# Block products of the second projections with the contraction pairs outside and the result's quarters inside, in chunks of up to seven pairs, and an entry that makes all blocks of u before their differences

## The chip, the cores and the metric

The kernel runs on one core of a Trainium2 chip. The metric is the device time of one execution in microseconds. A NeuronCore has TensorE (PE in the profile, with its weight loads as PEld), VectorE (DVE), ScalarE (ACT), GpSimd (POOL) and SyncE (SP), which here issues most transfers. Each engine works through its own list of instructions in order and waits where an instruction's inputs, or the buffer that it writes, are not ready.

## What is computed

A network of two blocks on x of 1024 rows (tokens) by 1024 columns, all in float32. The first block has two layers, each a mixer and an MLP; the second has a mixer and a gated feed-forward part. The change touches the two MLPs and the feed-forward part:

```python
# layer = 0, 1
u = x * (1.0 + scale) + shift
y = jnp.square(jax.nn.relu(u @ mlp_w1[layer] + mlp_b1[layer])) @ mlp_w2[layer] + mlp_b2[layer]
x = layer_norm(ALPHA * x + gate * y, ln_g[layer, 1], ln_b[layer, 1])
# second block
h = _causal_depthwise_conv(x @ w_up, conv_f_w, conv_f_b)
g, val = h[..., :2816], h[..., 2816:]
x = _layernorm(ALPHA2 * x + (jax.nn.silu(g) * val) @ w_down, ln2_g, ln2_b)
```

`mlp_w1` is 1024 by 4096, `w_up` 1024 by 5632; `mlp_w2` is 4096 by 1024 and `w_down` 2816 by 1024. In the text "first products" are those with `mlp_w1` and `w_up`, "second products" those with `mlp_w2` and `w_down`.

## The kernel before

Every float32 operand of a product is split into a high part (rounded, made by an ACT copy) and a low part (the rest, made by a DVE subtraction), and a product is three matmuls: high by high, high by low, low by high. One instruction list per engine is written out by hand in program order; what is issued earlier on an engine is done earlier on it.

**The entry** (`boundary`, L580) leads into each first product. It finishes the previous product with `last_sums`, normalises the rows, and then makes the transposed operand u, by halves h (512 tokens) and blocks kt (128 columns): `u_tile` (L570) is four transposes on PE into a `pb` bank, an affine ACT pass into `ur`, an ACT copy for the high part and a DVE subtraction for the low part. There are two `pb` buffers. The blocks of h = 1 are made while PE computes the h = 0 halves of the second and third of three weight tiles (`pss[1]`, `pss[2]`), at set places between the matmuls. After that come the h = 1 halves of all three, which need the blocks of h = 1, then a fourth weight tile (`fm_unit`), then the first block products (`FmProducts`). Those need, beside u itself, differences of the blocks of u: `diffs` (L1261) makes eight DVE operations and four ACT copies for one j of 0 to 3, out of the blocks j and j + 4 of both halves, into two tiles `t`. In the kernel before, `diffs` is issued right after the later of the two blocks, between the `u_tile` calls. Three entries have differences: those of the two MLPs and of the feed-forward part. In the last, the evacuations `evacs` hold a convolution, two DVE operations on 1024 columns each, and a product.

**The second products** (`TmProducts`, L1375) take the 2 by 2 block scheme with seven products instead of eight. Contraction blocks of 128 rows are taken in pairs. A chunk is a group of pairs over which a product is summed in PSUM before it is added to the result in SBUF (`acc`). There are 4, 3, 3 and 4 pairs in an MLP's chunks and 3, 3 and 3 in the feed-forward part's. For each chunk and each of the seven products j, `run` (L1466) goes over the four quarters t of the result (128 rows by 512 columns), and inside a quarter over the m pairs of the chunk, three matmuls each: 12 m matmuls for a product. `split` (L1433) makes the operands `he` of the next product beside this one (an ACT copy and a DVE subtraction for every two pairs, once for the weights `rw` and once for the hidden blocks `rh`), `sums` (L1417) the differences of weight blocks on DVE, four per chunk, and `add` (L1494) adds the finished halves of a product to `acc` on DVE: eleven additions of 1024 columns and six of 512 for a chunk. In the first chunk the first write of each quadrant of `acc` is an ACT copy instead, seven of 1024 and two of 512.

Beside the products run a side job, `residual_job` (L1504: load a row tile `zt`, two DVE operations, store, eight times), in the MLPs also `gated` (four weight tiles times the gate), and in the last chunk `ws.split` of the eight tiles for the entry after, and `add_residual` (L1519), which for each quadrant twice loads `zi`, in the MLPs multiplies `acc` by the gate on POOL, and adds `zi` on DVE. `step` (L1692) sets when. `begin` (L1648) makes the first loads and splits during the last pair of the first products.

SBUF tiles come from two pools: 21 buffers `W8` of 8 KB per partition (u, t, `he`, `rw`, `acc`, weight tiles) and 7 buffers `T4` of 4 KB (`rh`, `zt`, `zi`, `st`). PSUM has three buffers `ps` of two banks and two `pb` of one. A tile waits until a buffer is free.

Of the kernel before, what the change touches and what calls it, by code (L numbers as in the profile page):

```python
# [9 lines left out]
F32 = mybir.dt.float32  # L10
# [244 lines left out]
def tile_net(ctx: ExitStack, tc: tile.TileContext, x, wts, ada, adag, cols, rows, sfm, rgw, wup, wsp, out):  # L255
# [324 lines left out]
    def boundary(hs, wsx, xres, G, B, keys, evacs, spill=None, ops=None):  # L580
# [794 lines left out]
    class TmProducts:  # L1375
# [4 lines left out]

        def __init__(self, name, chunks, fresh):
            self.name, self.chunks, self.fresh = name, chunks, fresh
            self.n = 7 * len(chunks)
            self.w, self.h, self.ent = {}, {}, {}
            self.loaded, self.did = set(), set()
            self.nx = 0
# [4 lines left out]
        def weights(self, c, i, f):  # L1391

            if c >= len(self.chunks) or (c, i, f) in self.w:
                return
            ps = self.chunks[c]
            t = self.w[c, i, f] = W8("rw", (128, 4, 512), F32)
            u = _UNITS[self.name, 2 * ps[0]]
            src = wts[u:u + 2 * len(ps)].rearrange("(q two) p n -> two p q n", two=2)[i]
            nc.sync.dma_start(out=t[:, 0:len(ps), :], in_=src[:, :, f * 512:(f + 1) * 512])

        def load(self, g, k_):

            if g >= self.n or 2 * k_ >= self.m(g) or (g, k_) in self.loaded:
                return
            self.loaded.add((g, k_))
            c, j = divmod(g, 7)
            n = min(2, self.m(g) - 2 * k_)
            p = self.chunks[c][2 * k_]
            t = self.h[g, k_] = T4("rh").rearrange("p (q n) -> p q n", q=2)
            nc.sync.dma_start(out=t[:, 0:n, :], in_=d_h[p:p + n, (0, 6, 1, 2, 3, 4, 5)[j]].rearrange("q p n -> p q n"))  # L1410

        def w_of(self, g):

            c, j = divmod(g, 7)
            return self.w[(c,) + ((0, 0), (1, 0), (0, 0), (0, 0), (1, 1), (0, 1), (0, 0))[j]]

        def sums(self, g):  # L1417
            while self.nx <= min(g, self.n - 1):
                c, j = divmod(self.nx, 7)
                m = len(self.chunks[c])  # L1420
                x, b12, b22, b21 = [self.w[(c,) + k_][:, 0:m, :] if (c,) + k_ in self.w else None
                                    for k_ in ((0, 0), (0, 1), (1, 1), (1, 0))]
                if j == 2:
                    tt(x, b12, x, SUB)
                elif j == 3:
                    tt(x, b22, x, SUB)
                elif j == 4:
                    tt(b12, b22, b12, SUB)
                elif j == 6:
                    tt(x, b21, x, SUB)  # L1430
                self.nx += 1

        def split(self, g, k_):  # L1433

            if g >= self.n or 2 * (k_ % 2) >= self.m(g) or (g, k_) in self.did:
                return
            self.did.add((g, k_))
            q, n = 2 * (k_ % 2), min(2, self.m(g) - 2 * (k_ % 2))
            if k_ >= 2:
                self.sums(g)  # L1440
# [1020 lines left out]
```

## Time and profile before

| what | value |
|---|---|
| runs | 3709.20, 3709.82, 3719.66 us (median 3709.82) |
| profiled execution | 3706.28 us, its span 3704.4 us |
| PE busy | 3515.9 us, 95% of the span |
| DVE busy | 2663.2 us, 72% |
| ACT, POOL busy | 1469.9 us, 568.2 us |

The profile is one execution, seen by engine. A PE timeline merges matmuls that follow each other without a pause; the number in brackets is the idle time ahead of a row and what released it. A busy PE may still be slow, when its clock was granted at less than full speed. Averages over the span hide that the stages differ; so windows of a stage are read beside the timeline.

### The profile page before, as it was taken

To read this page: it belongs to the slowest core of one execution; us is meant where nothing else is said; L and a number is where in the kernel's file an instruction comes from. 1 tells how busy PE (TensorE), PEld (TensorE's weight loads), DVE (VectorE), ACT (ScalarE), POOL (GpSimd) and SP (SyncE) were. 2 spreads that over 40 slices of the span, in tenths; PEclk is the share of its full clock that TensorE was granted. 3 is DMA by queue.
4 is the path that set the end of the run, shared out by engine and by line. 5 is a ranking of instruction groups with operands and counts; after the bars stand their busy time and mean duration, and the time that the engine had idled before them with its cause. 6 is when DMAs were issued, how large, how long until landed. Compare 5 with 4: busy or idle time off the path is not lost. (4 is left out here: it accounts for less than half of the span.)

```text
span 3704.4 us, 43629 instructions
## 1 busy us (share of the span) xinstructions
PE 3515.9 (95%) x17098; PEld 2864.4 (77%) x17098; DVE 2663.2 (72%) x3640; ACT 1469.9 (40%) x1957; POOL 568.2 (15%) x415
## 2 busy tenths in 40 slices
PE   7999899999999999999899999999989999999997
PEld 5877778887877778888787888877768677777765
DVE  5574767868997764454647666798889677877897
ACT  4254353343335442443425334432413354444431
POOL 2002113300022000000202331002200013322002
PEclk9999999999999999999999999999989999999998
DMA  6343235465642222100122445574210323222662
GB/s 228 109 135 122 80 129 190 174 229 199 238 132 93 71 81 81 46 30 30 67 93 104 149 148 213 190 264 137 100 54 29 125 76 110 88 87 104 222 218 91
DMA packets 184160, 469.16 MB, mean 127 GB/s; under 512 B 15601, under 2 KB 20353, under 8 KB 183954
## 3 DMA queue, kind: packets, MB, share of 16 engines
q1 hardware_dynamic: 177378, 446.35, 34.1%
q0 software_dynamic: 6576, 20.03, 1.6%
q8 instruction: 134, 2.20, 0.2%
q14 instruction: 72, 0.59, 0.0%
HBM read 340.99 MB, written 125.32 MB: 126 GB/s over the span
## 5 line engine op out<-in xcount | busy, mean ns | idle before, releaser
L247 PE MATMUL ps<-u,wu 128*128 128x512 f32 x2880 | 755.6, 408 | 13.9 <-ACT u L577 5.3
L247 PEld LDWEIGHTS ps<-u,wu 128*128 128x128 f32 x2880 | 533.0, 192 | 140.1 <-issue 14.0
L247 PE MATMUL ps<-he 128*128 128x512 f32 x2442 | 582.9, 397 | 28.0 <-DVE he L305 21.7
L247 PEld LDWEIGHTS ps<-he 128*128 128x128 f32 x2442 | 460.6, 190 | 144.6 <-DVE he L305 33.0
L247 PE MATMUL ps<-t,we 128*128 128x512 f32 x1728 | 423.5, 393 | 5.4 <-DVE cc L305 5.3
L247 PEld LDWEIGHTS ps<-t,we 128*128 128x128 f32 x1728 | 323.4, 188 | 83.3 <-DVE cc L305 8.8
L247 PE MATMUL pb<-u,we 128*128 128x512 f32 x1152 | 281.9, 393 | 0.0
L247 PE MATMUL ps<-wu,u 128*128 128x256 f32 x1920 | 262.5, 291 | 16.4 <-DVE wu L218 14.3
L247 PEld LDWEIGHTS ps<-wu,u 128*128 128x128 f32 x1920 | 243.0, 193 | 27.4 <-DVE wu L218 15.1
L247 PEld LDWEIGHTS pb<-u,we 128*128 128x128 f32 x1152 | 216.2, 188 | 49.5 <-DVE we L305 0.2
L1446 ACT CAST he<-rw 128x1024 fp32r<-128x1024 f32 (+1 forms) x154 | 132.7, 911 | 240.4 <-DVE rw L305 227.0
L247 PE MATMUL ps<-pw,wu 128*128 128x512 f32 x816 | 211.3, 407 | 14.5 <-DVE xres L308 8.8
L1925 DVE TENSOR_REDUCE mx<-ps 128x1 f32<-128x128 f32 (+7 forms) x128 | 95.6, 755 | 173.5 <-PE ps L247 173.1
L305 DVE TENSOR_TENSOR we<-sf,we 128x512 fp32r<-128x512 f32 x192 | 153.9, 814 | 85.7 <-ACT we L1339 84.7
L305 DVE TENSOR_TENSOR he<-rw,he 128x1024 fp32r<-128x1024 f32 (+1 forms) x154 | 162.6, 1098 | 61.4 <-ACT he L1446 61.2
L1965 ACT ACTIVATE p<-ps 128x1024 f32<-128x1024 f32 (+7 forms) x128 | 82.9, 649 | 304.2 <-PE ps L247 288.4
L247 PEld LDWEIGHTS ps<-pw,wu 128*128 128x128 f32 x816 | 155.0, 194 | 51.5 <-DVE xres L308 9.2
L305 DVE TENSOR_TENSOR he<-rh,he 128x1024 fp32r<-128x1024 f32 (+1 forms) x154 | 165.9, 1079 | 18.6 <-ACT he L1446 18.4
L1446 ACT CAST he<-rh 128x1024 fp32r<-128x1024 f32 (+1 forms) x154 | 136.5, 911 | 88.5 <-DMA rh<-d_h 81.7
L305 DVE TENSOR_TENSOR acc<-acc,ps 128x1024 f32<-128x1024 f32 (+1 forms) x148 | 154.1, 1042 | 17.0 <-PE ps L247 16.6
L305 DVE TENSOR_TENSOR we<-wx,we 128x512 fp32r<-128x512 f32 x144 | 134.3, 934 | 44.5 <-ACT we L1339 44.5
L247 PE MATMUL pb<-he 128*128 128x512 f32 x666 | 158.5, 392 | 0.0
(395 smaller groups left out, 5847.7 us busy)
## 6 DMA issues: line engine op xcount, KB each, us to landing
st<-in_wts_dram SPq DMA_DIRECT2D x108, 512.0 KB, 3.4
rh<-d_h SPq DMA_DIRECT2D x105, 512.0 KB, 5.4
sf<-in_wts_dram SPq DMA_DIRECT2D x96, 512.0 KB, 6.6
d_h<-hx SPq DMA_DIRECT2D x37, 1024.0 KB, 5.1
d_h<-rr SPq DMA_DIRECT2D x111, 256.0 KB, 2.3
sta<-in_ada_dram SPq DMA_DIRECT2D x48, 512.0 KB, 3.6
rw<-in_wts_dram SPq DMA_DIRECT2D x28, 768.0 KB, 6.1
sta<-in_adag_dram SPq DMA_DIRECT2D x32, 512.0 KB, 3.9
```

Of the source, the lines that this page charges most:

```text
L247: return self.eng.matmul(out=out, lhsT=lhsT, rhs=rhs, **kw)
L305: (eng or dve).tensor_tensor(out=o, in0=a, in1=b, op=op)
L1446: act.copy(d[:, 0, 0:n, :], src)
L1925: dve.tensor_reduce(out=mx[:, t:t + 1], in_=ps[:, 0:n], axis=AX.X, op=ALU.max)
L1965: act.activation(out=p[:, 128 * i:1024], in_=ps[:, 128 * i:1024], func=AF.Exp)
```

## The change

At the three entries with differences the calls of `diffs` leave the place between the blocks of h = 1. The first is issued within the h = 1 half of the first weight tile, the second after it, the third after the second tile and its predecessor's evacuation, the fourth after the third tile.

In the second products the chunks become 7 and 7 pairs (MLPs) and 5 and 4 (feed-forward part). Inside a product the loop over the pairs is outside, two at a time (a unit), and the four quarters inside, so that a quarter gets 6 matmuls at a time, 3 in a unit of one pair, and all four quarters of a product end in its last unit. The additions to `acc` follow there, all at once. The order of the seven products changes so that those that accumulate in the two `aa` buffers (j = 0, 2, 4, 6) alternate with those in `cc` and the `pb` banks. Operands are split two units ahead and loaded four units ahead. The weights of a chunk come in two tiles per block, of up to four pairs. `begin` and `step` are spread anew over the units.

```diff
-                    if kt > 3 and ops is not None:
-                        diffs([[raws[h, kt - 4 + 4 * a] for a in range(2)] for h in range(2)], ops)
+        def diff(j):
+            if ops is not None:
+                diffs([[raws[h, j + 4 * a] for a in range(2)] for h in range(2)], ops)
+
         for c, _ in enumerate(fm_mms(pss[0], w[0], uT, 1)):
             if c % 2:
                 residual(4 + c // 2)
+            if c == 3:
+                diff(0)
+        diff(1)
         ws.split(ws.ng + 1, True, lo=pool)
         run(fm_mms(pss[1], w[1], uT, 1))
         evacs[0](pss[0])
+        diff(2)
         run(fm_mms(pss[2], w[2], uT, 1))
+        diff(3)
         evacs[1](pss[1])
...
+        def split(self, upto):
+            while self.ns < min(upto + 1, len(self.units)):
+                u = self.ns
+                (g, q), n = self.units[u], len(self.pairs(u))
+                c, j = divmod(g, 7)
+                if q % 2 == 0:
+                    self.sums(c, j, q // 2)
+                self.load(u)
...
+                for src in (self.w[(c,) + at + (q // 2,)][:, o:o + n, :], self.h.pop(u)[:, 0:n, :]):
+                    d = W8("he", (128, 2, 2, 512))
+                    act.copy(d[:, 0, 0:n, :], src)
+                    tt(d[:, 1, 0:n, :], src, d[:, 0, 0:n, :].bitcast(F32), SUB)
...
         def run(self, xres, step):
...
+                for q in range(0, m, 2):
+                    self.split(u + 2)
+                    self.load(u + 4)
+                    dw, dh = self.ent.pop(u)
+                    n = min(2, m - q)
+                    for t in range(4):
+                        s_ = slice(t * 128, (t + 1) * 128)
+                        for i in range(n):
...
+                    step(g, q // 2)
+                    u += 1
+                if on_a:
+                    for h in range(2):
+                        self.add(xres, c, j, 2 * h, 2, aa[h])
+                else:
+                    self.add(xres, c, j, 0, 2, cc[0])
+                    for t in (2, 3):
+                        self.add(xres, c, j, t, 1, cc[t - 1])
...
-            tp = TmProducts(f"w2_{l}", [[0, 1, 2, 3], [4, 5, 6], [7, 8, 9], [10, 11, 12, 13]], True)
+            tp = TmProducts(f"w2_{l}", [[0, 1, 2, 3, 4, 5, 6], [7, 8, 9, 10, 11, 12, 13]], True)
...
+        def step(g, q):
             c, j = divmod(g, 7)
+            last = g >= tp.n - 7
+            if g > 1 and not (last and j > 2):
+                for _ in range(2 if last or gate is None else 1):
+                    next(side_work, None)
+            if last:
+                if (j, q) == (3, 0):
+                    run(side_work)
+                if q == 1 and j > 3:
+                    add_residual(xres, gate, *((0, 1), (1, 1), (0, 0))[j - 4])
+                ws.split(min(ws.ng + 8, max(ws.ns, ws.ng + (0, 1, 2, 3, 3 + q, 7, 8)[j])))
...
-        tp = TmProducts("dn", [[0, 1, 2], [3, 4, 5], [6, 7, 8]], True)
+        tp = TmProducts("dn", [[0, 1, 2, 3, 4], [5, 6, 7, 8]], True)
```

## Rows read from the trace of the kernel before

**Rows 1.** The page, busy time: engine, us, share of the span, instructions.
```profile
PE 3515.9 (95%) x17098; PEld 2864.4 (77%) x17098; DVE 2663.2 (72%) x3640; ACT 1469.9 (40%) x1957; POOL 568.2 (15%) x415
```

**Rows 2.** Windows, one of 20 us in a three-pair chunk: busy time, clock, DMA.
```profile
900.00:920.00 20.00, 18.94 (x81) 14.55 (x80) 19.93 (x21) 3.95 (x6) 0.00 (x0) 1.00 0.64 233
```

**Rows 3.** Timeline of PE, first entry: start, length, matmuls, [idle before, releaser].
```profile
462.42 8.56 PE L247 MATMUL ps<-u,wu 128*128 128x512 f32 x36
470.81 0.60 PE L251 MATMUL pb<-ident,xres 128*128 128x128 f32 x4
...
480.00 0.66 PE L251 MATMUL pb<-ident,xres 128*128 128x128 f32 x4 [2.38 <-ACT ur L576]
...
495.79 25.57 PE L247 MATMUL ps<-u,wu 128*128 128x512 f32 x110 [0.23 <-DVE u L305]
521.21 2.96 PE L247 MATMUL ps<-u,we 128*128 128x512 f32 x12
```

**Rows 4.** Timeline of all engines at the first wait of that entry.
```profile
475.36 0.69 DVE L305 TENSOR_TENSOR tx<-ur 128x512 f32<-128x512 f32 x1
...
476.08 1.35 ACT L1274 CAST t<-tx 128x512 fp32r<-128x512 f32 x2 [1.36 <-DVE tx L305]
...
479.18 0.77 ACT L576 ACTIVATE ur<-pb,gb 128x512 f32<-128x512 f32 x1
479.22 1.29 DVE L305 TENSOR_TENSOR t<-ur,t 128x512 fp32r<-128x512 f32 x2
...
480.50 0.77 ACT L576 ACTIVATE ur<-pb,gb 128x512 f32<-128x512 f32 x1
```

**Rows 5.** Windows, 8 us around that wait (columns as in rows 2).
```profile
478.00:486.00 8.00, 4.77 (x17) 3.56 (x17) 7.17 (x13) 5.63 (x10) 0.00 (x0) 0.79 0.00 0
```

**Rows 6.** Timeline of PE, third entry: the same two places.
```profile
2985.84 8.33 PE L247 MATMUL ps<-u,wu 128*128 128x512 f32 x36
...
3044.45 2.92 PE L247 MATMUL ps<-u,we 128*128 128x512 f32 x12
```

**Rows 7.** Timeline of PE, start and end of the three stages of second products.
```profile
795.98 4.35 PE L247 MATMUL ps<-he 128*128 128x512 f32 x18
...
1075.42 8.48 PE L247 MATMUL ps<-wl,wu 128*128 128x512 f32 x36
...
2301.33 8.94 PE L247 MATMUL ps<-he 128*128 128x512 f32 x38
...
2587.56 8.53 PE L247 MATMUL ps<-wl,wu 128*128 128x512 f32 x36
...
3439.83 8.75 PE L247 MATMUL ps<-he 128*128 128x512 f32 x37
...
3632.49 12.69 PE L247 MATMUL ps<-wl,wu 128*128 128x512 f32 x54
```

**Rows 8.** Groups by shape, DVE, first stage of second products: busy us, mean ns.
```profile
L305 DVE TENSOR_TENSOR he<-rh,he 128x1024 fp32r<-128x1024 f32 x40 | 51.0, 1274 | 4.6 <-ACT he L1446 4.5
L305 DVE TENSOR_TENSOR acc<-acc,ps 128x1024 f32<-128x1024 f32 x36 | 43.8, 1217 | 3.5 <-PE ps L247 3.4
L305 DVE TENSOR_TENSOR rw<-rw 128x2048 f32<-128x2048 f32 x7 | 16.0, 2284 | 0.0
L305 DVE TENSOR_TENSOR acc<-acc,pb 128x512 f32<-128x512 f32 x22 | 15.0, 683 | 0.7 <-PE pb L247 0.7
```

**Rows 9.** Timeline of all engines, last chunk of the second stage.
```profile
2546.72 0.80 PE L247 MATMUL ps<-he 128*128 128x512 f32 x1 [3.54 <-DVE he L305]
...
2573.77 3.30 POOL L305 TENSOR_TENSOR acc<-acc,gate 128x1024 f32<-128x1024 f32 x1 [4.56 <-DVE acc L305]
2574.74 3.40 DVE L305 TENSOR_TENSOR he<-rh,he 128x1024 fp32r<-128x1024 f32 x1
```

**Rows 10.** Groups of the whole span, a convolution step of the feed-forward part.
```profile
L308 DVE SCALAR_TENSOR_TENSOR rr<-cc,col,rr 128x1023 f32<-128x1023 f32 x20 | 26.3, 1314 | 26.3 <-ACT rr L2304 26.3
```

More of the change, by code (lines that the diff above doesn't have):

```diff
@@ L1383, in __init__ @@
             self.n = 7 * len(chunks)
+            self.units = [(g, q) for g in range(self.n) for q in range((self.m(g) + 1) // 2)]
             self.w, self.h, self.ent = {}, {}, {}
-            self.loaded, self.did = set(), set()
-            self.nx = 0
+            self.nl = self.ns = 0
         def m(self, g):
@@ L1391, in weights @@
         def weights(self, c, i, f):
-            if c >= len(self.chunks) or (c, i, f) in self.w:
+            if c >= len(self.chunks) or (c, i, f, 0) in self.w:
                 return
[L1395 to L1431, printed above, removed]
@@ L1449, in beside @@
-        def beside(self, g, t):
-            if t == 0:
-                self.split(g + 1, 2)
-                self.split(g + 1, 3)
-            elif t < 3:
-                self.split(g + 1, t - 1)
-            else:
-                self.sums(g + 2)
-        def fetch(self, g, t):
-            c, j = divmod(g, 7)
-            if t > 1:
-                self.load(g + 2, t - 2)
-            elif t == 0 and 1 < j < 6:
-                self.weights(c + 1, *((0, 0), (1, 0), (0, 1), (1, 1))[j - 2])
+            for x in range(0, len(self.chunks[c]), 4):
+                ps = self.chunks[c][x:x + 4]
+                t = self.w[c, i, f, x // 4] = W8("rw", (128, 4, 512), F32)
+                u = _UNITS[self.name, 2 * ps[0]]
+                src = wts[u:u + 2 * len(ps)].rearrange("(q two) p n -> two p q n", two=2)[i]
+                nc.sync.dma_start(out=t[:, 0:len(ps), :], in_=src[:, :, f * 512:(f + 1) * 512])
@@ new lines, in pairs, with load @@
+        def pairs(self, u):
+            g, q = self.units[u]
+            return self.chunks[g // 7][2 * q:2 * q + 2]
+        def load(self, upto):
+            while self.nl < min(upto + 1, len(self.units)):
+                ps = self.pairs(self.nl)
+                j = (0, 1, 2, 3, 4, 6, 5)[self.units[self.nl][0] % 7]
+                t = self.h[self.nl] = T4("rh").rearrange("p (q n) -> p q n", q=2)
+                nc.sync.dma_start(out=t[:, 0:len(ps), :], in_=d_h[ps[0]:ps[0] + len(ps), j].rearrange("q p n -> p q n"))
+                self.nl += 1
@@ L1472, in run @@
                     aa = [PSUM(), PSUM()]
[L1473 removed]
+                if j in (1, 5):
                     cc = [PSUM(), PB(), PB()]
[L1475 to L1492 removed]
@@ new lines, in run @@
+                on_a, start = j % 2 == 0, j in (0, 1, 5)
+                os_ = [aa[t // 2][:, t % 2 * 512:t % 2 * 512 + 512] if on_a else
+                       cc[0][:, t * 512:(t + 1) * 512] if t < 2 else cc[t - 1] for t in range(4)]
+                for q in range(0, m, 2):
[6 more added lines that the diff above has]
+                        for i in range(n):
+                            first, last = start and q + i == 0, q + i == m - 1
+                            hh, hl, wh, wl = dh[:, 0, i, s_], dh[:, 1, i, s_], dw[:, 0, i, :], dw[:, 1, i, :]
+                            pe.matmul(out=os_[t], lhsT=hh, rhs=wh, start=first, stop=False, skip_group_check=not start)
+                            pe.matmul(out=os_[t], lhsT=hh, rhs=wl, start=False, stop=False, skip_group_check=not start)
+                            pe.matmul(out=os_[t], lhsT=hl, rhs=wh, start=False, stop=last, skip_group_check=not start)
+                    if q == 0:
+                        if j in (0, 1):
+                            self.weights(c, 1, 1 - j)
+                        elif j in (5, 6):
+                            self.weights(c + 1, 0, j - 5)
+                    step(g, q // 2)
+                    u += 1
```

81 lines of the change are left out of this document (25 added, 56 removed).

## The prediction

> **What bounds the kernel.** I read the page's busy times first: PE is busy 95% of the span [rows 1], so a gain can only come from places where PE stands still or runs at its lower clock. The PE timeline of the stages that the change touches comes next. A matmul of 512 columns takes 0.231 us from start to start: 110 of them fill 495.79 to 521.21 [rows 3].
>
> At the first entry PE goes from 462.42 to 521.21, 58.8 us [rows 3]. The work in it is 192 matmuls (four weight tiles of 48), 44.4 us, and eight groups of four transposes. A group moves what follows by about 0.35 us: the matmuls ahead of it end by their pitch at 462.42 + 36 x 0.231 = 470.74, and of its 0.60 us [rows 3] a good part overlaps. That makes 2.8 us, and 58.8 - 47.2 = 11.6 us are lost. The timeline says how: PE waits 2.4 us for an ACT pass `ur` [rows 3], twice, and 1.7 us a third time, and after a wait the granted clock averages 0.79 [rows 5], part of the time at 1.2 instead of 2.4 GHz. ACT is late because `diffs` stands in its list between two blocks of u: its copy waits 1.36 us for DVE's `tx`, and the next block's `ur` starts only at 479.18 [rows 4], while PE has run out of `pb` buffers. The pattern repeats at the other two entries; the third takes 2985.84 to 3044.45, 58.6 us, so 11.4 lost [rows 6], and the second lies between them.
>
> The three stages of second products take 279.4, 286.2 and 192.7 us [rows 7]. Their matmuls (1176, 1176 and 756) need 271.7, 271.7 and 174.6 us at 0.231. Lost: 7.8, 14.6 and 18.0 us, 40 in all. There DVE is the engine that is late: busy 19.9 of 20 us in a three-pair chunk [rows 2], and PE waits for `he` from DVE [rows 9]. So some 75 us, 2% of the time, lie within reach of this change, and no more.
>
> **The entries, part by part.** Nothing is removed; 32 DVE operations and 16 ACT copies per entry move. Once out of the way, a block of u costs ACT 1.32 us, start of one `ur` to the next [rows 4], and PE asks for one every 1.0 to 1.7 us (three or six matmuls and the transposes), so ACT just keeps up and the 11.6 us go. The cover for the moved work: a `diffs` takes DVE from 475.36 to 480.51, 5.15 us [rows 4], four take 20.6. By PE's work the last block of u is ready some 14 us after the first group of transposes at 470.81 [rows 3], at about 485, and the four would end near 506. What needs them is product 1 of the block products. PE gets there after the three h = 1 halves (16.6 us from about 484), the fourth tile (11.1) and product 0 (2.8): at about 514. So the differences themselves are covered by 8 us. What is late next is what queues behind them on DVE: four operations on the hidden pair, about 2.7 us at 0.68 each (the 512-column row of [rows 8]), then the first block-product weights, needed at about 511. 506 + 2.7 + 0.7 is 509.4; POOL's weight split beside it can stretch DVE by 2 us or so (below). I price the two MLP entries at 1 us lost each, between 0 and 3. The feed-forward entry has three convolved tiles and a product behind the same queue: six operations of 1.31 us [rows 10] and one of 1.22, 9.1 us more, so its first block product would be 4 to 6 us late; taken 5, between 2 and 9. Gain: 10.6 + 10.6 + 6.4 = 27.6 us, from 20 to 34.
>
> **The second products, part by part.** PE's matmuls stay the same in number. A quarter now changes after 6 matmuls, where it was 9 or 12; I price a change at nothing, since in the three-pair chunks, with a change every 9, the granted clock is 1.00 [rows 2] and all of PE's gaps there have a DVE releaser. A PSUM bank cycled too often is what the Trainium skill warns of (TensorE: Matmul & The Clock Gate, "A second HAM failure mode: psum-queue depth-cycling"): small idles between the groups let the clock drop. This trace does not show it at 9; it is rival E.
>
> DVE loses additions: an MLP had 44 of 1024 columns and 24 of 512 in four chunks, and has 22 and 12 in two. 22 x 1.217 + 12 x 0.683 = 35 us each [rows 8]; the feed-forward part loses half of that, 17.5. Splits and weight differences keep their total columns.
>
> What this does to PE follows by chunk. Before, three pairs: PE 7 x 36 x 0.231 = 58.2 us; DVE seven times two subtractions of 1.25 and two of 0.68 (27.0), additions 11 x 1.22 + 6 x 0.68 = 17.5, weight differences 4 x 1.71 (three quarters of 2.284) = 6.8, side job about 11: 62, over PE's time, as the window shows. In the last chunk: four pairs, 77.6 us for PE; 35 + 17.5 + 9.1, eight tiles for the next entry 10, six residual additions 7.3, and 13 us by which POOL's gate stretches DVE: 92. After, seven pairs: PE 135.8 us; DVE in the first chunk 7 x (6 x 1.25 + 2 x 0.68) = 62, additions 17.5 less 10 that go to ACT, differences 16, side job 12: 98, with much room. In the last chunk 62 + 17.5 + 16 + 14 + 10 + 7.3 + 13 = 140: still a little over, and crowded into products 4 to 6, where three of the eight tiles and the residuals fall. Each operand is ready two units, about 11 us, ahead, which takes up most of that. A wait for a late `zi`, as behind the 3.54 us of [rows 9], can still come through. I leave 2.5 us lost in the first stage and 4 in the second. Feed-forward part: first chunk 97 us for PE, about 92 for DVE with the convolutions left over; last chunk 77.6 against 79: 6 lost. Gain: 5.3 + 10.6 + 12 = 28 us; the ends are 0, if the last chunk loses all that is lost now, and 40.
>
> The stretch: a subtraction of 1.22 took 3.40 us beside a POOL multiplication of 3.30 [rows 9], 2.2 more. The Trainium skill says more (SBUF — State Buffer, "Who interferes with whom"): of the two, whichever issues second is blocked for the whole instruction. By that, six multiplications would cost DVE 20 us, and the last chunk would lose some 5 us more.
>
> The new waits: `add` of a finished product now stands on DVE ahead of the split for two units later. Behind PE's last matmul come 2.4 us of additions, up to 2.3 of differences [rows 8] and 2.5 of subtractions, 7.2 against 11 us of cover. In the first chunk ACT's copies into `acc` stand there likewise. Both residual additions of the last quadrant come after the end, as one did before; POOL twice 3.3 and the additions end at about 9 us, where the next entry's PE needs a PSUM buffer at 8.3 (36 matmuls): 1 us either way, 0 taken.
>
> **Sum.** 27.6 + 28 = 55.6 us off the profiled execution's own 3706.3: 3650.7. It lies 3.5 us under the median of the runs shown, within their spread; I add 2 and forecast 3653, own range 3634 to 3672.
>
> **Rivals.** A, the forecast: 0.55. B: the last chunk keeps its losses, because the additions come in bursts and residuals, tiles and gates still fall in three products; gain there 0 to 13, so 3665 to 3680. For it: the tally of 140 against 136; against: the units in hand. 0.20. C: the entries give back what they gain, differences or the queue behind them being late by 8 to 11 us everywhere, the products as forecast: 3706 - 28, about 3680. Against it stands 8 us of cover. 0.06. Both B and C: 3700 to 3712, no change. 0.08. D, slower: the buffers. Four `acc`, eight `rw` (two per block now), six `he` for three units, one row tile and two tiles of the next entry are 21, all there are. If in fact fewer than six `he` find room, only one unit is made ahead; the odd unit of one pair covers 2.8 us, where the next head needs a difference and two subtractions with their copies, about 6, and the additions delay the one after by 2.4 beyond its 5.5. Some 4 us for each of 42 products less what is lost now: 3706 - 28 - 40 + 168 = 3806, or 3722 with half of it. It decides from the first chunk on, wherever PE waits at each head. 0.09. E: PE loses its clock between quarters; at 0.79 [rows 5], 718 us of matmuls would take 190 more, 3850 and up. 0.02.
>
> **Chances and range.** About 0.3%, 11 us, is what a measurement here can tell from no change. Faster: A, B, C, 0.81. Same: 0.08. Slower: D, E, 0.11. The range runs from A's lower end to past B and C, 3632 to 3688, and leaves out the same and slower cases.
>
> **What would show it.** Entries right: no PE wait for `ur` between the transposes, 47 to 50 us from the first u matmul to the first block product, 52 in the third; wrong: a wait on `t` or `we` from DVE at the first products. Second products right: stages of about 274, 276 and 181 us, DVE with idle time in the first chunk, the waits that stay lying in the last three products; wrong: waits for `he` at each product's head (D), or a granted clock under 1.00 with no wait (E).

## The result and the profile after

The changed kernel takes 3737.96 us in the median (3733.77 to 3740.43), the kernel before beside it 3710.32 us; the ratio is 1.0068, 95% interval 1.0049 to 1.0087. It is slower, by 28 us. The forecast was 3653 us, and the time lies above the range too.

The profiled execution took 3739.17 us, its span is 3737.5. The page's busy times, as in [rows 1]:

```profile
PE 3535.4 (95%) x17098; PEld 2878.9 (77%) x17098; DVE 2603.7 (70%) x3541; ACT 1468.7 (39%) x1943; POOL 572.5 (15%) x415
```

DVE has lost 60 us of work, and the kernel is slower all the same. (The additions to `acc` fell by 87 us, as the prediction reckoned; e1 below, the new entries alone, has 23 us more DVE time than before, and why is seen at the entries.) Where, the PE timeline tells: I take the start of the first matmul of each kind (`u,wu`, then `we`, `he`, `wl,wu`) as the border of a stage. All runs of the study stand in one table, the three places of each stage one after the other. "Ratio" is to the kernel before on the same chip.

| kernel | us | ratio (95%) | entries | first products | second products |
|---|---|---|---|---|---|
| before | 3710 | | 58.8 / 58.9 / 58.6 | 274.8 / 271.8 / 395.4 | 279.4 / 286.2 / 192.7 |
| changed | 3738.0 | 1.0068 (1.0049–1.0087) | 51.6 / 51.4 / 57.1 | 277.2 / 272.8 / 398.8 | 294.4 / 307.5 / 196.3 |
| e1 | 3703.3 | 0.9975 (0.9965–0.9984) | 51.5 / 51.3 / 57.2 | 277.2 / 274.1 / 398.1 | 281.4 / 286.1 / 195.2 |
| e2 | 3751.4 | 1.0099 (1.0078–1.0119) | 58.8 / 58.9 / 58.9 | 274.8 / 271.4 / 397.8 | 294.1 / 306.4 / 196.0 |
| e3 | 3668.1 | | old | 274.9 / 272.0 / 396.9 | 271.2 / 271.1 / 180.3 |
| e4 | 3662.6 | | old | 274.8 / 271.4 / 395.9 | 271.1 / 271.0 / 179.4 |
| e5 | 3713.8 | 0.9999 (0.9990–1.0009) | as changed | as changed | 293.4 / 292.8 / 190.5 |
| e6 | 3722.3 | 1.0021 (1.0011–1.0030) | as changed | as changed | 289.9 / 299.9 / 195.1 |
| e7 | 3690.4 | | as changed | as changed | 279.8 / 291.5 / 176.9 |
| e8 | 3702.2 | | as changed | as changed | 285.0 / 287.0 / 197.9 |
| e9 | 3693.1 | 0.9945 (0.9931–0.9960) | as changed | as changed | 280.6 / 293.2 / 180.1 |
| e10 | 3668.2 | 0.9879 (0.9865–0.9894) | as changed | as changed | 271.9 / 275.0 / 180.8 |
| e11 | 3737.5 | 1.0064 (1.0048–1.0081) | 50.4 / 50.3 / 53.2 | 281.5 / 278.1 / 400.5 | 294.8 / 306.6 / 195.4 |
| e12 | 3719.9 | 1.0024 (1.0014–1.0033) | as changed | as changed | 287.7 / 300.7 / 195.2 |
| e13 | 3726.8 | 1.0039 (1.0025–1.0054) | 47.9 / 47.9 / 54.0 | 277.1 / 273.1 / 399.7 | 293.7 / 307.3 / 193.9 |
| e14 | 3737.9 | 1.0065 (1.0050–1.0080) | 51.9 / 51.8 / 57.1 | 276.9 / 273.3 / 399.2 | 293.6 / 307.1 / 196.4 |
| e15 | 3702.0 | 0.9970 (0.9959–0.9981) | as changed | as changed | 283.7 / 283.3 / 193.8 |
| e16 | 3666.1 | 0.9874 (0.9859–0.9889) | 47.9 / 47.9 / 47.6 | 281.7 / 277.4 / 407.6 | 272.7 / 275.7 / 180.4 |
| e17 | 3656.2 | 0.9858 (0.9843–0.9873) | 47.9 / 47.7 / 54.1 | 277.3 / 273.7 / 399.1 | 271.0 / 274.7 / 180.7 |
| e18 | 3647.6 | 0.9829 (0.9812–0.9845) | 47.9 / 47.9 / 54.1 | 277.1 / 273.6 / 399.7 | 270.6 / 270.2 / 180.3 |

("As changed" is within 1.2 us. e3, e4, e7 and e8 leave work out and so compute something else; they stand without a ratio.) From before to changed: entries -16.2 us, the first products behind them +6.9, the second products +39.8; that is 30.6 of the 33.1 us between the two spans (3704.4 and 3737.5). So the entries brought about a third of what I had said, and the second products, forecast to give 28 us, took 40.

**The second products.** The windows of the first stage, first to 920 us, then the rest (columns as in rows 2):

```profile
790.88:920.00 129.12, 129.12 (x560) 104.99 (x559) 94.68 (x85) 55.69 (x65) 1.58 (x3) 1.00 0.65 226
920.00:1085.28 165.28, 151.15 (x620) 120.50 (x618) 118.86 (x100) 55.16 (x63) 18.34 (x6) 0.94 0.55 186
```

In the first chunk PE never stops, where before it did at that time of the stage [rows 2]. In the last it stands 14 us, the granted clock averages 0.94, so that part of the time it is at the lower of its two levels, 1.2 instead of 2.4 GHz, and there DVE is busy only 119 of 165 us. This is the reading that matters: PE is late, and the engine that I had called the bound stands still too. The waits of the second stage (waiter, what it waited for: us in total, times, longest): first DVE's on `zi` in the kernel before, then DVE's and the DMA queue's in the changed kernel:

```profile
DVE acc L305 <- DMA zi<-d_zm: 6.5, 2, 4.0
...
DVE he L305 <- ACT he L1451: 45.6, 24, 6.9
DVE acc L305 <- DMA zi<-d_zm: 20.8, 6, 5.0
DVE wu L218 <- ACT wu L216: 8.8, 1, 8.8
DVE zt L308 <- DMA zt<-d_zm: 6.6, 2, 6.0
...
DVE zw L305 <- DMA zw<-in_wts_dram: 3.9, 1, 3.9
...
SPq L1527 <- DVE he L305: 11.5, 4, 9.3
SPq L1527 <- DMA zi<-d_zm: 10.9, 3, 4.5
```

and one such place there, PE, DVE and SP:

```profile
2594.63 1.22 PE L247 MATMUL ps<-he 128*128 128x512 f32 x2 [8.91 <-ACT he L1451]
...
2583.89 1.23 DVE L305 TENSOR_TENSOR acc<-acc,zi 128x1024 f32<-128x1024 f32 x1 [5.02 <-DMA zi<-d_zm]
2589.05 1.22 DVE L305 TENSOR_TENSOR acc<-acc,zi 128x1024 f32<-128x1024 f32 x1 [3.94 <-DMA zi<-d_zm]
2590.19 2.29 DVE L305 TENSOR_TENSOR rw<-rw 128x2048 f32<-128x2048 f32 x1
2593.66 1.23 DVE L305 TENSOR_TENSOR he<-rw,he 128x1024 fp32r<-128x1024 f32 x1 [1.19 <-ACT he L1451]
...
2578.89 6.61 SPq L1527 DMA_DIRECT2D zi<-d_zm  x2
```

DVE's list holds the residual addition ahead of the weight difference (`rw`) for the next operand. DVE waits 5.02 us for the first `zi`; SP's two loads of `zi` take 6.61 us to issue, because the second wants a buffer: it is through at 2585.50, just after DVE's addition of the first has ended at 2585.12. So DVE waits another 3.94. Then the difference, ACT's copy, DVE's subtraction, and PE, which the page puts down to ACT, has stood 8.91 us for two DMA waits in DVE's list.

The row of `wu` is a third kind of wait on a DMA. It is the split of the next entry's first weight tile; second stage, SP and ACT:

```profile
2478.72 0.34 SPq L1679 DMA_DIRECT2D d_wl<-zw  x1
2479.16 0.38 SPq L1675 DMA_DIRECT2D zw<-in_wts_dram  x1
2479.63 3.44 SPq L184 DMA_DIRECT2D st<-d_hx  x3
...
2486.38 1.04 ACT L216 CAST wu<-st 128x1024 fp32r<-128x1024 f32 x1 [10.27 <-DMA st<-d_hx]
```

The load of `st` stands in SP's list behind the store of a gate tile `zw`, and that store waits until DVE has multiplied the tile. ACT then waits 10.27 us for `st`, DVE 8.8 for ACT, and PE 3.65 behind them (4.12 at the same place of the first stage). DVE's waits for `zi`, `zt` and `zw` and this one come to 23.5, 40.1 and 22.6 us in the three stages.

The scaling of the residual waits likewise. Third stage, DVE and SP:

```profile
3555.05 1.23 DVE L308 SCALAR_TENSOR_TENSOR zt<-zt,xrow 128x1024 f32<-128x1024 f32 x1 [4.66 <-DMA zt<-d_zm]
...
3549.05 0.78 SPq L1514 DMA_DIRECT2D zt<-d_zm  x1
```

The load was issued at 3549.05; the operation on it is the next entry of DVE's list, since where the changed `step` takes two side steps per unit, a load and its use can have nothing between them. Four of the eight tiles of that stage wait so, 4.5 to 5.3 us each.

**The entries.** The waits for `ur` between the transposes are gone, as forecast. In their place stands one wait at the first block product, in each of the three. DVE and POOL in the middle of the differences, and PE behind them:

```profile
494.31 2.90 DVE L305 TENSOR_TENSOR tx<-ur 128x512 f32<-128x512 f32 x1
497.25 0.69 DVE L305 TENSOR_TENSOR tx<-ur,tx 128x512 f32<-128x512 f32 x1
497.97 1.80 DVE L305 TENSOR_TENSOR ur<-ur,tx 128x512 f32<-128x512 f32 x1
499.69 1.78 DVE L305 TENSOR_TENSOR ur<-ur 128x512 f32<-128x512 f32 x1
501.39 2.39 DVE L305 TENSOR_TENSOR t<-tx,t 128x512 fp32r<-128x512 f32 x2
...
494.19 2.47 POOL L218 TENSOR_TENSOR wu<-st,wu 128x1024 fp32r<-128x1024 f32 x1 [34.08 <-ACT wu L216]
497.93 1.29 POOL L305 TENSOR_TENSOR wx<-sf 128x512 f32<-128x512 f32 x1 [1.27 <-DMA sf<-in_wts_dram]
499.30 1.62 POOL L305 TENSOR_TENSOR wx<-wx,sf 128x512 f32<-128x512 f32 x1
...
513.65 4.93 PE L247 MATMUL ps<-u,we 128*128 128x512 f32 x12 [3.57 <-ACT we L1346]
518.42 2.94 PE L247 MATMUL pb<-t,we 128*128 128x512 f32 x12
```

A subtraction of 0.69 us takes 2.90 beside POOL's 2.47. PE waits 3.57 us (3.31 and 9.10 at the other two), and then pays again: its next 12 matmuls take 4.93 us, where the 12 after them take 2.94. The windows of these two groups show the granted clock (before the DMA share) at 0.64 and 1.00, so in the first it is for part of the time at the lower level:

```profile
513.65:518.40 4.75, 4.69 (x12) 3.42 (x13) 3.56 (x5) 4.69 (x7) 3.19 (x3) 0.64 0.80 297
518.42:521.20 2.78, 2.78 (x14) 2.26 (x13) 2.71 (x3) 1.21 (x3) 2.78 (x2) 1.00 0.43 160
```

### The profile page after: what moved, and what is told of

It reads as the page before. It is cut to its first block, busy times and chain, and to the rows that moved or that the text cites. A ratio compares the mean times of both kernels' runs of the same rounds, so it can differ in the third digit from the quotient of the medians.

```text
span 3737.5 us, 43460 instructions
## 1 busy us (share of the span) xinstructions
PE 3535.4 (95%) x17098; PEld 2878.9 (77%) x17098; DVE 2603.7 (70%) x3541; ACT 1468.7 (39%) x1943; POOL 572.5 (15%) x415
## 5 line engine op out<-in xcount | busy, mean ns | idle before, releaser
L247 PE MATMUL ps<-he 128*128 128x512 f32 x2442 | 599.8, 403 | 51.9 <-ACT he L1451 38.5
L247 PEld LDWEIGHTS ps<-he 128*128 128x128 f32 x2442 | 469.4, 193 | 171.9 <-ACT he L1451 44.4
L247 PE MATMUL ps<-pw,wu 128*128 128x512 f32 x816 | 213.4, 410 | 13.8 <-DVE xres L308 8.0
L247 PEld LDWEIGHTS ps<-pw,wu 128*128 128x128 f32 x816 | 156.2, 196 | 51.3 <-DVE xres L308 8.4
L247 PE MATMUL pb<-he 128*128 128x512 f32 x666 | 166.5, 397 | 0.0
L247 PE MATMUL ps<-u,we 128*128 128x512 f32 x576 | 146.4, 404 | 16.1 <-ACT we L1346 16.0
```

The costliest lines, as they stand in the source:

```text
L247: return self.eng.matmul(out=out, lhsT=lhsT, rhs=rhs, **kw)
```

## Experiments

**Are the parts separate, and is it the product order or the side work?** Theory 1: the side work (scaling of the residual `zt`, its additions `zi`, gate, `zw`) stands late in DVE's and ACT's lists, and the order itself costs nothing. Theory 2: the order costs (bursts of additions, quarters that change every 6 matmuls).

e1, the first two hunks of the change alone:

```diff
-                    if kt > 3 and ops is not None:
-                        diffs(...)
+            if c == 3:
+                diff(0)
+        diff(1)
...
```

> The kernel before with the new order at the three entries alone. If the two parts of the change are independent, the traces give -7.2, -7.5 and -1.5 us for the entries and +2.5, +1.0 and +3.4 us behind them in the first products: 9 us less than before, about 3701. If what is slower in the second products comes from the entries (buffers or loads shifted by the new order), this kernel is slower than before.

e2, all but these two hunks:

```diff
+                    if kt > 3 and ops is not None:
+                        diffs(...)
-            if c == 3:
-                diff(0)
-        diff(1)
...
```

> The changed kernel with the old order at the entries. If the parts are independent: the three stages of second products take some 294, 308 and 196 us as in the changed kernel, 40 us more than before, about 3747. If the second products suffer from the entries, about 3710.

The entries alone give 0.25%, the products alone cost 1.0%; the stages that each part concerns are those of the changed kernel to within 1.3 us, the others those of the kernel before to within 2.6. The parts don't touch.

e3, on e2, and e4, the same on the kernel before, leave out the residual's work: no `zt`, no `zi` and no gate on POOL; `zw` and the splits for the next entry stay:

```diff
         for i in (2 * th, 2 * th + 1):
+            continue
...
-            yield from job
+            yield
```

> As e2, but the residual is left out: no residual job beside the second products, no zi loads, no gate multiplications and no residual additions (the residual is missing in the result, and the gate on all but the last eight blocks). Theory 1, waits for side loads (zt, zi) in DVE's list delay the operands: the stages fall to about 275, 277 and 179 us, 40 us under e2's plus what e4 gains. Theory 2, the pairs outside cost by themselves (additions in bursts, operands made in lumps behind them): the stages stay over those of e4 by 15 us or more in the first two.

> The kernel before with the same work left out as in e3, so that e3 and e4 differ by the order of the second products alone. Theory 1: stages of about 275, 278 and 182 us, a little over those of e3, since the additions that e3 saves still load DVE in the three-pair chunks. Theory 2: clearly under e3's.

Without the residual's work both orders run at PE's floor in the first two stages: 271.2 and 271.1 us, and 271.2 is 1176 matmuls of 0.2306. The window of e3's first stage:

```profile
798.39:1069.57 271.18, 271.18 (x1177) 220.96 (x1176) 177.91 (x160) 111.30 (x130) 2.86 (x8) 1.00 0.51 175
```

PE never waits, the clock is 1.00. Theory 2 falls: neither bursts nor quarters cost anything here, with DVE busy 178 of 271 us (and with 213, e10 below). The third stage, 180.3 and 179.4, still holds 3 us of PE waits near its start and the clock that they cost; e7 comes to 176.9, so the loss of that stage is known to some 3 us only. Above these times the kernel before loses 8, 15 and 13 us, the changed one 23, 36 and 16, all of it with side work.

**What of the side work?** Theory P: seven buffers are shared by `rh`, `zt`, `zi`, the weights' `st` and up to three rows, and are too few. Theory Q: load and use fall in the same unit.

e5, e6, e7, e8, e12, each on the changed kernel:

```diff
# e5
-                    self.load(u + 4)
+                    self.load(u + 3)
# e6 (zw: the same order of load and use as before, a step later)
             nc.sync.dma_start(out=d_zm[t * 128:(t + 1) * 128, :], in_=z)
+            if t < 7:
+                z = load(t + 1)
             yield
# e7
-            yield from job
+            yield
# e8
-            z = T4("zi").rearrange("p (i n) -> p i n", i=2)
-            nc.sync.dma_start(out=z, ...)
-            tt(x, x, z, ADD)
# e12
-            tt(x, x, gate_row[gate]..., MUL, pool)
+            tt(x, x, gate_row[gate]..., MUL)
```

> The changed kernel, with the activations' loads of the second products (rh) issued three units ahead instead of four, so that one buffer less of their pool is held by rh and the side transfers (zt, zi, which share the pool) find one sooner. Theory P (the side transfers are late because the pool is full): the wait of the load queue for freed buffers in the last chunks (23.8 us in the third stage) shrinks, the zi waits of VectorE (8, 21, 3 us in the three stages) go to about half, and the three stages fall from 294/307/196 to about 285/293/190, so about 3712 us. Theory Q (they are late because load and use come in the same unit of PE, whatever the pool): nothing moves, 3738 us within 4; and if rh itself comes late now, some us more.

> The changed kernel, with the load of each zt tile (and of the gate's tile) issued one side step before the one that computes on it, in the step that stores the one before it; the number of side steps is the same. Now a unit of the last chunk takes two steps, so that load and use can fall between the same two units. Theory Q: VectorE's zt waits (5.4, 6.0, 19.5 us in the three last chunks) go, and with them the TensorE waits that follow; stages about 288/300/180 instead of 294/307/196, so about 3708 us. Theory P: the loads are as late as before for want of buffers, or a buffer is held longer and zi is later still: 3738 us or some 5 more.

> The changed kernel, with the residual's scaling (the zt tiles: load, two VectorE operations, store; its row sums) left out, so the residual goes in unscaled; the zi loads and additions and the gate's multiplication on GpSimd stay. If the zt waits are the cause: the third stage, in which they are 19.5 us, falls from 196 to about 181, the first two (5.4 and 6.0 us of zt waits) only from 294/307 to about 288/300, so about 3710 us. If zi and the gate are the cause, or the pool that all share: with zt gone zi has its buffers, and the first two stages fall to about 275, so about 3670 us.

> The changed kernel, without the loads and additions of zi, so the residual is left out of the result; the zt tiles, the gate and its multiplication on GpSimd stay. If zi's waits are the cause: the first two stages (8 and 21 us of VectorE waits for zi) fall from 294/307 to about 284/284, the third (3 us) hardly, so about 3703 us. If zt's are: all but some 5 us of the loss stay, 3730 us.

> The changed kernel with the gate's multiplications (eight in each of the two first stages) on VectorE instead of GpSimd. If GpSimd's two in a row (5.8 us, VectorE beside it stretched to 2.5 and 3.4 us) make the additions late: VectorE gains some 5 us at each pair in spite of 2.3 us more of its own, the first two stages about 284/295 instead of 294/307, 3715 us. If VectorE waits for zi's transfer anyway: the stages gain nothing or lose some 2 us, 3738 to 3742 us. The third stage, without a gate, moves in neither.

One buffer fewer held by `rh` gives 14.7 us in the second stage, where DVE's waits on `zi` fall from 20.8 to 10.1, and 5.8 in the third, 1 in the first: buffers are part of it. The earlier `zt` load gives 4.5, 7.7 and 1.1. I had looked for 16 in the third stage: with two steps per unit a load still has only one unit, and it stands in SP's list behind a store that waits for DVE, so DVE's waits on `zt` there stay (15.7 us, from 19.5). e6 also makes the job shorter, though I had written that the number of steps stays: a `zt` tile takes two steps instead of three. Leaving out the scaling takes 14.6, 16.1 and 19.4 us off, leaving out `zi` 9.4, 20.5 and nothing (1.7 more); the sums, 24, 37 and 18, are near the losses of 23, 36 and 16. So there are two sources, and they add. For e7 the theory of the `zt` waits alone gave only 6 and 7 us in the first two stages, their length in the list of DVE's waits. The rest isn't a faster `zi`: DVE waits 8.1 and 22.1 us for it in e7, where it was 8.0 and 20.8. What is gone with `zt` is the wait of 8.8 us for `wu` in each of the two stages, since without the scaling the gate's four tiles `zw` fall into the first chunk, and the load of `st` no longer stands behind their stores. So e7's share is that of the whole row of side steps, not of `zt` alone. The gate off POOL gives 7 us in each of the two stages that have one.

e9, on the changed kernel: one side step per unit everywhere, begun one product earlier.

```diff
-            if g > 1 and not (last and j > 2):
-                for _ in range(2 if last or gate is None else 1):
-                    next(side_work, None)
+            if g > 0 and not (last and j > 2):
+                next(side_work, None)
```

> The changed kernel with the side work (zt, then zw) spread as in the kernel before: one step per unit of TensorE (5.5 us) instead of two in the last chunk (and in the whole third stage), and from the second product on instead of the third, so that it ends at the same place. Theory Q (load and use in the same unit are what makes it late): the job's share of the loss, 14.6, 16.1 and 19.4 us by the run without it, falls to about half, stages 287/299/186 instead of 294/307/196, about 3712 us. Theory P (the seven buffers that rh, zt, zi, the weights' st and three rows share are too few, whatever the spacing): 3738 us within 5.

It gives 13.8, 14.4 and 16.2 us, about as much in the first two stages as leaving the scaling out, and brings the third to e3's time. I had expected 26 us in all; it is 44 in the three stages. DVE's wait for `wu` is gone, and its waits for `zt` are 1.5, 0.9 and 0 us; those for `zi` stay, 8.0 and 21.3 in the first two stages. Spacing and the earlier start, with the same seven buffers, turn a loss of 0.7% into a gain of 0.55%; how much is due to either of the two wasn't run apart.

e10 adds e5, and loads `zi` a unit before its addition:

```diff
+                    if q == 0:
+                        zs.append(load_residual(*b))
+                    else:
+                        add_residual(xres, gate, *b, zs.pop())
...
```

> The changed kernel with three repairs of the side work at once: one step per unit as above, rh a unit later as above, and zi loaded one unit (5.5 us) before its addition. If buffers and spacing are all of the loss: the three stages near 276/279/184 (their floors are 271/271/180), about 3688 us, 1% faster than the kernel before. If the repairs get into each other's way (zi held a unit longer takes the buffer that rh freed): no better than rh alone, 3714 us.

3668 us, 1.2% under the kernel before. First stage:

```profile
797.70:1069.63 271.93, 271.93 (x1177) 220.77 (x1176) 213.22 (x184) 110.94 (x128) 19.93 (x9) 1.00 0.62 221
```

PE never waits, with DVE's work the same 213 us as in the changed kernel (213.5). The stages are 271.9, 275.0 and 180.8; DVE's waits for `zi` in the first two are 0 and 3.6 us, and those for `wu`, `zt` and `zw` are gone. So the changed kernel's loss came from when the loads of its side work arrive, not from an amount of work. What the earlier `zi` gives without e5's buffer wasn't run.

**Is the order worth anything?** e15 is e1 with the same mending of `zi`, and `rh` a quarter later:

```diff
-            if t > 1:
-                self.load(g + 2, t - 2)
...
+            if t == 3:
+                self.load(g + 2, 0)
+            elif t == 0:
+                self.load(g + 1, 1)
...
-                if t == 3 and j in (2, 5, 6):
...
+                if t % 2 and j in (2, 5, 6):
...
+                    if t == 1:
+                        zs.append(load_residual(*b))
+                    else:
+                        add_residual(xres, gate, *b, zs.pop())
...
```

> The kernel before with the new entries, its old product order (quarters outside, pairs inside, chunks of three and four), and the side work mended as far as it needs it: zi loaded two quarters (5.5 us) before its addition, rh one quarter later; its steps are already one in two quarters. If the order itself is worth nothing (both orders ran at their floor without side work): the losses fall from 8/15/13 to about 2/4/5, 279/286/193 to about 273/275/184, near 3678 us, within 10 us of the new order mended (3668 us). If the new order's fewer additions on VectorE matter under side work: it stays over 3690 us.

It stays at 3702 us. The first stage, first as a window, then all that PE waits for in it:

```profile
793.04:1076.69 283.65, 275.41 (x1177) 221.33 (x1176) 244.63 (x217) 110.62 (x128) 21.05 (x10) 0.99 0.59 207
```

```profile
PE ps L247 <- DVE acc L305: 4.0, 3, 2.0
PE ps L247 <- DVE he L305: 4.0, 4, 2.3
```

DVE waits for no `zi` there; it is busy 245 of 284 us, where the new order has 213 of 272. So with the side work mended the new order is 11.7, 8.3 and 13.0 us shorter, 33 in all. The 31 us of DVE work between the two windows are the likely reason; it isn't shown apart, since the orders differ in chunks and in how far ahead operands are made too. One reserve: ACT's waits for `rh` in this stage grew to 45 us from 24 in e1, so the old order may have a better mending than mine.

**The entries.** e11 puts the first block weights, e14 the second evacuation ahead of the last differences; e13 takes POOL from beside them.

```diff
# e11
         diff(2)
+        if fp is not None:
+            fp.split(2)
# e14
+        evacs[1](pss[1])
         diff(3)
-        evacs[1](pss[1])
# e13 (and the three sums of the first block: pool -> pool if q else None)
-        ws.split(ws.ng + 1, True, lo=pool)
+        ws.split(ws.ng + 1, True, lo=None if ops is not None else pool)
```

> The changed kernel with the first three weight pieces (we) of the block products made between the third and the fourth group of differences instead of behind everything at the entry. If their place in ScalarE's and VectorE's lists makes TensorE wait at the first block product (3.6, 3.3 and 9.1 us): these waits go, the clock stays up, entries 48/48/50 instead of 51.6/51.4/57.1 and the first products 273 instead of 277 in the first stage, about 3720 us. If the differences themselves, stretched beside GpSimd, are what ends last: the wait moves behind the first product (t instead of we) and the sum of both stages stays within 2 us each, 3736 us.

> The changed kernel with the second evacuation of each entry ahead of the fourth group of differences instead of behind it. If ScalarE's list is the cause (it waits 3.0 us for the fourth group at 505.6 with an evacuation behind that could run, 2.2 us of work): weights and third evacuation come 2 us earlier, the wait at the first block product 3.6 -> 1.5 us, clock back earlier, 3730 us; in the third entry, where the convolution also puts work on VectorE, less. If the differences are what ends last: within 2 us, 3737 us.

> The changed kernel with GpSimd's four operations beside the differences of each entry (the fourth weight's low half and the first block's three sums) given to VectorE, so that the differences run alone. If GpSimd beside them is the cause (the third group took 10.6 us instead of 5.2): VectorE has 3.3 us more to do and loses 5.4 us of stretch, the last difference ends some 2 us earlier, and the wait at the first block product falls from 3.6 and 3.3 us to about 1.5: both stages together -3 us each, 3730 us. If the place in the lists is the cause (evacuations and weights behind all differences): nothing moves or it grows by 3 us: 3738 to 3745 us.

e11 only moves the wait: entries 1.2, 1.1 and 3.9 us shorter, the stage behind 4.3, 5.3 and 1.7 longer (PE waits 4.09 us for an evacuation at 522). e14 does nothing. e13 gives 11 us: DVE's list, then PE:

```profile
496.82 0.68 DVE L305 TENSOR_TENSOR tx<-ur 128x512 f32<-128x512 f32 x1
...
501.89 0.69 DVE L305 TENSOR_TENSOR tx<-ur 128x512 f32<-128x512 f32 x1
...
505.75 1.29 DVE L305 TENSOR_TENSOR t<-ur,t 128x512 fp32r<-128x512 f32 x2
...
513.36 2.58 PE L247 MATMUL ps<-u,we 128*128 128x512 f32 x10 [1.44 <-DVE we L305]
```

The third group takes 5.1 us (496.82 to 501.89) instead of 10.6. The last ends at 507.0 instead of 510.1, and counted from each run's own start of the entry (463.44 and 462.06) at 43.6 instead of 48.0 us, though DVE also does the weight split of 1.22. The wait falls from 3.57 to 1.44, and the ten matmuls behind it take 2.58 us, at a granted clock of 1.00. POOL beside the differences was the cause in the two MLP entries. In the third the wait falls from 9.10 to 6.07 us and stays there (6.03 in e17), behind the convolutions: with the weights ahead of them (e11) PE waits 5.29 us at the same place for a convolution on DVE.

**Joined.** e16 is e10 with e11, e13 and e14; e17 is e10 with e13 alone; e18 is e17 with e12.

```diff
# e16: e10 + e11 + e13 + e14
         diff(2)
+        evacs[1](pss[1])
+        if fp is not None:
+            fp.split(2)
# e17: e10 + e13
+        ws.split(ws.ng + 1, True, lo=None if ops is not None else pool)
# e18: e17 + e12
-            tt(x, x, gate_row[gate]..., MUL, pool)
+            tt(x, x, gate_row[gate]..., MUL)
```

> The changed kernel with its side work mended as in e10 (3668 us), and the entries with all three repairs: no GpSimd beside the differences, the second evacuation and the first weights ahead of the fourth group. If the three are what the entries still lose (waits 3.6, 3.3, 9.1 us and 2 us each at half clock behind): 3654 us. If they only move the wait as e11 did: 3668 us within 3.

> The changed kernel with the side work mended as in e10 (3668 us) and the differences alone as in e13 (11 us below the changed kernel), without the two moves of e11 and e14. If the two are independent as the entries and the products were: 3668 - 11 = 3657 us. If VectorE's 3.3 us more at each entry come out again behind it: 3665 us.

> As the run before, with the gate's multiplications on VectorE instead of GpSimd. If GpSimd's stretch is a cost of its own: a few us less in the second stage (275 us, floor 271), 3654 us. If it cost only because the additions behind it were late already: the same time within 2 us, or the second stage 2 us longer for VectorE's own 9 us of multiplications.

e17 is the sum of its parts (3656 for 3657). e16 is 10 us worse by its median (6 by the ratios, since the two ran on different chips), and its entries and first products together are 10 us longer: the moves of e11 and e14 hurt once the differences run alone. The gate on DVE still gives 8.6 us by the medians, 4.5 of them in the second stage, which is now at the floor:

```profile
2277.41:2547.62 270.21, 270.21 (x1177) 221.00 (x1176) 212.58 (x190) 110.63 (x127) 2.12 (x4) 1.00 0.64 224
```

DVE does six multiplications more there and is busy for 213 us as before (212.6, in e17 213.4): the stretch beside POOL had cost it as much as the multiplications do. PE gains where it still waited, 2.7 us in e17's second stage; the first, in which it no longer waited, goes from 271.0 to 270.6. e18, 3647.6 us, beats the kernel before by 1.7% (0.9812 to 0.9845).

## Why the prediction was wrong

**What bounds the kernel**: half right. For the order of before e15 bears it out: all that PE waits for in its first stage is `he` and `acc` from DVE. For the changed kernel it failed: what bounds its last chunk is not DVE's work but DMA waits in DVE's list. DVE was busy 119 us in the window from 920 to the stage's end, where the tally had 140 for the last chunk, so as a count of work the tally was even too high.

**The second products**: the step that failed is the tally of the two chunks, "98, with much room" and "140: still a little over", in which the side job stands with 12 and 14 us of busy time and with no wait. In its place the runs show DMA waits of 23.5, 40.1 and 22.6 us in DVE's list, from two sources. One is a line of the diff that I read past, `range(2 if last or gate is None else 1)`: two steps of the job per unit put a load and its use next to each other, and the next weights' load behind a store that waits; e9, without it and begun a product earlier, gets 44 us back. The other is `add_residual`, which loads `zi` and adds it in one go. It did so before too, and DVE waited 6.5 us for it in the second stage; in the changed kernel it is 20.8, and without `zi` (e8) the first two stages are 9 and 21 us shorter. The sentence "Each operand is ready two units, about 11 us, ahead, which takes up most of that" fell with it: two DMA waits in a row, 5.02 and 3.94, with a difference of 2.29, a copy and a subtraction behind them, use up the 11 us. I did write that a wait for a late `zi` can come through, and left 2.5 and 4 us for all that is lost; it was 23 and 36. With the side work spaced and loaded ahead, the terms come out: 274, 276 and 181 us were forecast, e10 has 271.9, 275.0 and 180.8. From the kernel before to e10 the second products gain 30.5 us, where I had 28; that needs the mending, which is no part of the change. The additions themselves fell by 87 us of DVE time, as reckoned. The stretch by POOL's gate, priced at 13 us, comes to about 8 by an estimate from e17 and e18: six multiplications of 1.22 us on DVE leave its busy time 0.9 us lower.

**A change of quarter at nothing**: right (e3, e10: clock 1.00, no wait). By the Trainium skill's rule on depth-cycling (TensorE: Matmul & The Clock Gate, "A second HAM failure mode: psum-queue depth-cycling"), which I had put into rival E, small idles between the groups of matmuls put the clock at risk; e3 and e10 have no such idles in their first stages, so no run here shows it.

**The entries**: the waits for `ur` went, and 506 us for the end of the differences, 43.6 after the start of the entry at 462.42, is what e13 shows without POOL (43.6). Two terms were too small. "POOL's weight split beside it can stretch DVE by 2 us or so" measured 5.5 us: the split alone did stretch it by 2.2, but POOL has four operations there, and the three sums weren't counted; and a wait at the first product brings half clock behind it, 2 us each, which I hadn't priced. Lost against my 47.2 us of work, with the 2 us behind: some 6 each instead of 1 in the MLP entries; in the third, 57.1 for a forecast of 52. Net gain 9.3 us (16.2 less 6.9) for 27.6. (The second entry before took 58.9 us, a little over the other two and not between them; nothing hangs on it.)

**The rivals.** B had the right place, the last chunk, and half of the mechanism: residuals and gates crowded there did cost (e8, e12), bursts of additions did not (e3). Its ends were a gain of 0 to 13; it was a loss of 40. C was partly true: the entries gave back two thirds. D's buffers were the wrong pool: the 21 large tiles sufficed, PE standing nowhere in the first chunk; the seven small ones did not (e5). That 3738 lies between D's two times, 3722 and 3806, is luck, since the waits at each product's head that they were worked out from didn't come. E did not occur: the clock is 1.00 in the first chunk. No rival held that the side work itself would come later than before, and that is why the range missed.

## What to carry to other kernels

Count a side job not by its busy time but by what lies between each load and its use in the list of the engine that uses it: here two steps per slot of 5.5 us, against one and an earlier start, cost 44 us with the same buffers. Look too at what stands behind a store in the loading queue: a load there waits for the engine whose result is stored. When an engine that was the bound becomes idle and the kernel is slower, look for DMA waits in its list, then for the load's buffer, then for the queue that issues it; the wait that the page shows at TensorE names only the last link. And before a change of order is judged, run both orders without the side work: it tells in two runs whether the order or its surroundings cost the time.

## What the runs showed of the hardware

A 512-column subtraction of DVE, 0.69 us by itself, took 2.90 us beside a POOL operation of 2.47, and 1.80 and 1.78 beside POOL's of 1.29 and 1.62. Each of the three began just after the POOL operation (0.12, 0.04 and 0.39 us) and ended 0.55 us after its end, so each lost what was left of it. The Trainium skill (SBUF — State Buffer, "Who interferes with whom") says that whichever of the two issues second is blocked for the whole of the other's instruction; these rows agree, and the 2.2 us of [rows 9], where DVE began 0.97 us after POOL's 3.30, agree as well. I had not expected the price of moving work from DVE to POOL to be above that of doing it on DVE: e13, e12 and e18 all gain by bringing it back.

A wait of 3.57 us at PE cost 5.6: the 12 matmuls behind it took 4.93 us instead of 2.94, with the granted clock at 0.64 in their window.
